# Router queries from fp32 weights and an fp32 router input instead of split halves

## The chip, the cores and the metric
The kernel runs on one core of a Trainium2 chip. The metric is the device time of one launch in microseconds. A core has five engines that work side by side, each in the order of its own instructions: TensorE (PE, with PEld for its weight loads), VectorE (DVE), ScalarE (ACT), GpSimd (POOL) and SyncE (SP), which here only issues transfers.

## The reference, cut to what matters
A hybrid encoder block (gated linear attention beside differential attention, merged, with a residual) is followed by PEER, a retrieval layer over 128 x 128 single-neuron experts. There are 256 tokens of width 2048, all in float32. The part that matters is PEER, on `xb = rmsnorm(hs, g_ffn)`:

```
qb = (xb @ w_q).reshape(TB, 8, 2, 128)              # router queries, 8 heads
s = einsum('thpc,hpnc->thpn', qb, sub_keys)         # scores of 128 keys, twice
sv, si = top_k(s, 16)
cand = sv[:, :, 0, :, None] + sv[:, :, 1, None, :]  # 16 x 16 pairs
cv, ci = top_k(cand, 16);  eidx = ...               # 16 experts of each head
g = softmax(cv)
a = gelu(einsum('thkd,td->thk', u_tab[eidx], xb))   # 128 rows of 2048 per token
out = einsum('thkd,td'..., g * a, v_tab[eidx])
```

The final output is `rmsnorm(hs + out)`.

## The kernel before
The whole program is straight-line code. A planner with a timing model of its own puts it in order ahead of the run and sets the waits, so each engine has one fixed order; blocks marked high priority are put ahead of others that are ready at the same planned time. Tiles with one tag share a few buffers.

**Projections.** `proj` computes 256 columns of a product with a 2048-row weight in two halves of 8 row blocks each, 1 MB per half. `load_half` fetches a half on SP's queue (L174), ScalarE rounds it to `hi` in fp32r (L185), and DVE, or the engine given as `lo_eng`, subtracts to get `lo` (L186). The activations are kept as the same pair of halves. PE multiplies three pairs for each block: high by high, high by low, low by high (L200 to L202), 256 token columns at a time, so 96 products for one call.

**The router.** The output projection `w_o` (L215 to L217) ends the attention part; its result `hs` is transposed on PE (L665) block by block, and `hg[k]`, the router input before its row scaling, is made as a high half by ScalarE (L667) and a low half by DVE (L668). `queries(h)` then runs for each of the eight heads: `proj` with `w_q`, ScalarE's copy to `pqt` (L783), fp32 score products with the transposed keys (L790), ScalarE's scaled copy to `s0` or `sS1` (L792), and `route(0, h)` for the first 128 tokens. For head 0 DVE makes `lo`, for heads 1 to 7 POOL. The first half of a weight lies in the `raw` tag (3 buffers); the second in the `ring` pool (3 buffers) for heads 0 and 1, in four quarter tiles of the old `s1` buffers for heads 2 to 4, and in `raw` for heads 5 to 7.

**Routing.** `route` finds the top 16 twice on DVE (L708 to L712), adds the pairs (`cand`, L723), takes the top 16 of them, and turns them into row numbers with a few small operations (`hl` L729 and L730, `ohx` L734, L736 on POOL, L737, L739). ScalarE's exponent (L743) takes `cv`.

**Lookups.** `gather_dots` fetches one row of the `u` table for each of 128 tokens, 1 MB, with an indirect transfer on POOL's queue (L751), and DVE multiplies it by `xb` and sums (L754). There are 256 of these, half into `g` tiles of `ring`, half into `gr` tiles that share the tag `raw` with the query weights. `route(1, h)` for the second 128 tokens is interleaved. `weights_of(0)` (GELU, L763) follows the last dot of the first 128 tokens; `build_w0` then builds a one-hot weight array W0 on ScalarE and PE (L815 to L821), while DVE goes on with the dots of the second 128. `split_w` makes the halves `wb` of W0 (L897, L898).

**The dense stage.** With W0 and W1 built, a product over the whole `v` table runs to the end, with the last 576 columns by gathers (L884, L887).

Of the kernel before, what the change touches and what calls it, by code (L numbers as in the profile page):

```python
# [10 lines left out]
F32 = mybir.dt.float32  # L11
F32R = mybir.dt.float32r
# [3 lines left out]
AF = mybir.ActivationFunctionType  # L16
ALU = mybir.AluOpType
# [3 lines left out]
P = 128  # L21
D = 2048
KT = D // P
T = 256
# [16 lines left out]
def block_kernel(ctx: ExitStack, tc: tile.TileContext, A: dict, out: bass.AP):  # L41
    nc = tc.nc

    def pool(name, bufs=1, space=None, side=None, c=ctx):
        kw = {}
        if space is not None:
            kw["space"] = space
        if side is not None:
            kw["side"] = side
        return c.enter_context(tc.tile_pool(name=name, bufs=bufs, **kw))  # L50
# [5 lines left out]
    wp = pool("wp", side="right", c=wpc)  # L56
# [7 lines left out]
    s2p = pool("s2p", c=ph1)  # L64
    ph0 = ExitStack()
    s1p = pool("s1p", c=ph0)

    def pm(shape=(P, N)):
        return pmain.tile(list(shape), F32, tag="pm", name="pm")

    def pa(shape):
        return paux.tile(list(shape), F32, tag="pa", name="pa")
# [76 lines left out]
    for k in range(KT):  # L149
        ps = pa([P, N])  # L150
        for i, (xt, n) in enumerate(xs):
            nc.tensor.matmul(ps[:, i * P:i * P + n], lhsT=xt[:, k * P:(k + 1) * P], rhs=sc[i], start=True, stop=True)
        g = vec[:, gm + k:gm + k + 1]
# [6 lines left out]
    def block_of(c0):  # L160
        return (c0 - 32 if c0 > OFF_LR else c0) // 256

    def load_half(w, c0, kh, ncol=256, lo_eng=None, ring=None):

        src = w[block_of(c0), kh]
        if ring is None:
            parts = [wp.tile([P, 8, ncol], F32, tag="raw", name="raw", bufs=3)]
        elif isinstance(ring, list):
            parts = [s1p.tile([P, 2, ncol], F32, tag=f"s1_{t}", name="raws") for t in ring]
        else:  # L170
            parts = [ring.tile([P, 8, ncol], F32, tag="g", name="rawg")]
        n = 8 // len(parts)
        for i, raw in enumerate(parts):
            nc.sync.dma_start(raw, src[:, i * n:(i + 1) * n, :])  # L174
        res = []
        for q in range(2):
            hi = wp.tile([P, 4, ncol], F32R, tag="hi", name="hi", bufs=3)
            lo = wp.tile([P, 4, ncol], F32R, tag="lo", name="lo", bufs=3)
            m = min(n, 4)
            with tc.high_priority():  # L180
                for i in range(4 // m):
                    k0 = 4 * q + i * m
                    raw = parts[k0 // n][:, k0 % n:k0 % n + m, :]
                    ks = slice(i * m, (i + 1) * m)
                    nc.scalar.activation(hi[:, ks], raw, AF.Copy)  # L185
                    (lo_eng or nc.vector).tensor_sub(lo[:, ks], raw, hi[:, ks].bitcast(F32))  # L186
            res.append((hi, lo))
        return res

    def proj(w, c0, act, n, evac, lo_eng=None, ring=None):  # L190

        ps = [pm((P, n)) for _ in range(2)]
        for kh in range(2):
            for q, (hi, lo) in enumerate(load_half(w, c0, kh, lo_eng=lo_eng, ring=ring and ring[kh])):
                for kk in range(4):
                    k = kh * 8 + q * 4 + kk
                    ah, al = act[k][:, 0, :n], act[k][:, 1, :n]
                    for b in range(2):
                        wh, wl = hi[:, kk, b * P:(b + 1) * P], lo[:, kk, b * P:(b + 1) * P]
                        nc.tensor.matmul(ps[b], lhsT=wh, rhs=ah, start=(k == 0), stop=False)  # L200
                        nc.tensor.matmul(ps[b], lhsT=wh, rhs=al, start=False, stop=False)  # L201
                        nc.tensor.matmul(ps[b], lhsT=wl, rhs=ah, start=False, stop=(k == KT - 1))  # L202
        for b in range(2):
            evac(b, ps[b])

    def proj_tokens(w, c0, act, evac):

        ps = [pm((P, 256)) for _ in range(2)]
        for kh in range(2):
            for q, (hi, lo) in enumerate(load_half(w, c0, kh)):  # L210
                for kk in range(4):
                    k = kh * 8 + q * 4 + kk
                    for tt in range(2):
                        ah, al = (act[k][:, i, tt * P:(tt + 1) * P] for i in range(2))
                        nc.tensor.matmul(ps[tt], lhsT=ah, rhs=hi[:, kk], start=(k == 0), stop=False)  # L215
                        nc.tensor.matmul(ps[tt], lhsT=ah, rhs=lo[:, kk], start=False, stop=False)
                        nc.tensor.matmul(ps[tt], lhsT=al, rhs=hi[:, kk], start=False, stop=(k == KT - 1))  # L217
        for tt in range(2):
            evac(tt, ps[tt])
# [9 lines left out]
    for kh in range(2):  # L229
        raw = bt.tile([P, 8, 32], F32, tag="ow", name="lraw", bufs=4)  # L230
        nc.sync.dma_start(raw, w_lr[kh])
        hi = wp.tile([P, 8, P], F32R, tag="hi", name="lhi", bufs=3)
        lo = wp.tile([P, 8, P], F32R, tag="lo", name="llo", bufs=3)
# [4 lines left out]
        for kk in range(8):  # L238
            k = kh * 8 + kk
# [82 lines left out]
    def gla_head(h):  # L322
# [19 lines left out]
        def ev_r(j):  # L342
# [6 lines left out]
            return f  # L349

        proj(w_in, OFF_GQ + h * 256, hT, T, ev_q)
        proj(w_in, OFF_GK + h * 256, hT, N, ev_k)


# [74 lines left out]
        for m in (2, 3):  # L429
# [4 lines left out]
            Qb[m] = t_  # L434

        proj(w_in, OFF_GV + h * 512, hT, N, ev_v(0))
        proj(w_in, OFF_GV + h * 512 + 256, hT, N, ev_v(1))

# [203 lines left out]
    ring = pool("ring", bufs=3, side="right", c=ringc)  # L642
# [3 lines left out]
    hg = [None] * KT  # L646
    gf = vrow["g_ffn"]
    w_o = A["c_w_out"]
    for j in range(8):
        xr = bt.tile([P, 2, 256], F32, tag=f"b{j % 2}", name="xr")  # L650
        nc.sync.dma_start(xr, A["x"][0].rearrange("(a p) c -> p a c", p=P)[:, :, j * 256:(j + 1) * 256])

        def ev_o(tt, ps, j=j, xr=xr):
            cs = slice(j * 256, (j + 1) * 256)
            nc.vector.tensor_add(hs[:, tt, cs], ps, xr[:, tt, :])
            jk = bt.tile([P, 256], F32, tag="ow", name="jk", bufs=4)
            nc.scalar.activation(jk, hs[:, tt, cs], AF.Square, accum_out=ssq[:, tt, j:j + 1])

        proj_tokens(w_o, j * 256, yT, ev_o)
        for b in range(2):  # L660
            k = 2 * j + b
            g = vec[:, gf + k:gf + k + 1]
            p2 = pa([P, T])
            for tt in range(2):
                nc.tensor.transpose(p2[:, tt * P:(tt + 1) * P], hs[:, tt, k * P:(k + 1) * P], ident)  # L665
            hg[k] = s2p.tile([P, 2, T], F32R, tag=f"s2_{k}", name=f"hg{k}")
            nc.scalar.activation(hg[k][:, 0, :], p2, AF.Copy, scale=g)  # L667
            nc.vector.scalar_tensor_tensor(hg[k][:, 1, :], p2, g, hg[k][:, 0, :].bitcast(F32), op0=ALU.mult,  # L668
                                           op1=ALU.subtract)

    for tt in range(2):
        nc.gpsimd.dma_start(xb[:, tt, :], A["g_ffn"].to_broadcast([P, D]))
# [99 lines left out]

    w_q = A["c_peer_w_q"]

    wait = [(None, ring), (None, ring), (None, [4, 5, 6, 7]), (None, [8, 9, 10, 11]), (None, [12, 13, 14, 15])] + [None] * 3
    eis = {}

    def queries(h):
        qt = bt.tile([P, 2, T], F32, tag=f"b{2 + h % 2}", name="pqt")

        def ev_pq(b, ps):
            with tc.high_priority():
                nc.scalar.activation(qt[:, b, :], ps, AF.Copy)  # L783
        proj(w_q, h * 256, hg, T, ev_pq, lo_eng=nc.vector if h == 0 else nc.gpsimd, ring=wait[h])
        s0 = rp.tile([P, 2, P], F32, tag="sS0", name="sS0", bufs=2)
        with tc.high_priority():
            for tt in range(2):
                ps = pa([P, 2, P])
                for p in range(2):
                    nc.tensor.matmul(ps[:, p, :], lhsT=qt[:, p, tt * P:(tt + 1) * P], rhs=skT[h // 2][:, 2 * (h % 2) + p, :],  # L790
                                     start=True, stop=True)
                nc.scalar.activation(s0 if tt == 0 else sS1[:, h], ps, AF.Copy, scale=rst[tt])  # L792
            eis[0, h] = route(0, h, s0)

    sub_keys(0)
    queries(0)
    for b in range(1, 4):
        sub_keys(b)
    for tt in range(2):
        nc.vector.scalar_tensor_tensor(xb[:, tt, :], hs[:, tt, :], rst[tt], xb[:, tt, :], op0=ALU.mult, op1=ALU.mult)  # L800
    for h in range(1, 8):
        queries(h)
# [250 lines left out]
```

## Time and profile before

| what | value |
|---|---|
| median of 3 runs | 2611.87 us (2609.34 to 2613.95) |
| the profiled execution | 2616.36 us, span 2614.6 us |
| PE busy | 1889.1 us (72%) |
| DVE busy | 2132.0 us (82%) |
| ACT busy | 1106.8 us (42%) |
| POOL busy | 1266.1 us (48%) |
| mean DMA rate over the span | 252 GB/s |

The busy shares are means over stages that differ: PE is busy in 90% or more of nearly every slice until about 1200 us and again from about 2000 us on, DVE from about 1200 on. The stage table among the rows below is therefore the view to start from.

### The profile page before, as it was taken

The numbers are of one execution on the slowest core, as the hardware profiler recorded it, in microseconds if no ns is written. First come the engines' busy times: TensorE is split into PE (matmuls) and PEld (weight loads), VectorE is DVE, ScalarE is ACT, GpSimd is POOL, SyncE is SP. The second block draws the span as 40 slices with busy tenths as digits, with TensorE's granted clock in tenths as the row PEclk, the third lists the DMA queues.
The fourth block names the chain that finished last, engine by engine and source line by source line (L and its number), as shares of the span: only waits on it lengthen the run. The fifth ranks groups of instructions, "written<-read, shape, count | busy, mean of one in ns | idle before, by whom it ended". The sixth has DMA issues, their size and how long they took to land. (4 is left out here: it accounts for less than half of the span.)

```text
span 2614.6 us, 37107 instructions
## 1 busy us (share of the span) xinstructions
PE 1889.1 (72%) x13809; PEld 1835.5 (70%) x13809; DVE 2132.0 (82%) x2921; ACT 1106.8 (42%) x2076; POOL 1266.1 (48%) x989
## 2 busy tenths in 40 slices
PE   8999999999999999997500000143006999999997
PEld 7999999999999999997500000132005888999897
DVE  4778877557777775559999999996978899999998
ACT  4565554345655544443200000698006344444444
POOL 1333310000110001028876888885856777777775
PEclk9999999999999999998855555566558999999999
DMA  4445445554444465656699899997993788889886
GB/s 160 146 147 178 146 148 199 187 181 164 165 157 166 167 237 180 227 198 213 227 350 347 322 375 422 421 421 298 418 357 117 263 304 301 315 302 306 302 300 240
DMA packets 110913, 658.38 MB, mean 252 GB/s; under 512 B 14514, under 2 KB 17132, under 8 KB 53116
## 3 DMA queue, kind: packets, MB, share of 16 engines
q0 software_dynamic: 59216, 348.40, 35.2%
q1 hardware_dynamic: 51312, 307.45, 33.8%
q8 instruction: 108, 1.77, 0.3%
q14 instruction: 73, 0.60, 0.1%
q10 hardware_dynamic: 204, 0.17, 0.0%
HBM read 652.78 MB, written 2.10 MB: 250 GB/s over the span
## 5 line engine op out<-in xcount | busy, mean ns | idle before, releaser
L186 DVE TENSOR_TENSOR lo<-raw,hi 128x1024 fp32r<-128x1024 f32 x354 | 453.2, 1281 | 242.7 <-ACT hi L185 240.9
L202 PE MATMUL pm<-hT,lo 128*128 128x256 f32 (+1 forms) x2048 | 577.9, 285 | 7.9 <-DVE lo L186 7.9
L200 PE MATMUL pm<-hT,hi 128*128 128x256 f32 (+1 forms) x2048 | 581.8, 285 | 0.0
L201 PE MATMUL pm<-hT,hi 128*128 128x256 f32 (+1 forms) x2048 | 581.6, 285 | 0.0
L185 ACT ACTIVATE hi<-raw 128x1024 fp32r<-128x1024 f32 x374 | 395.9, 1059 | 363.3 <-PE pm L201 292.5
L202 PEld LDWEIGHTS pm<-hT,lo 128*128 128x128 f32 x2048 | 384.9, 189 | 10.7 <-DVE lo L186 9.0
L200 PEld LDWEIGHTS pm<-hT,hi 128*128 128x128 f32 x2048 | 386.0, 188 | 0.3
L201 PEld LDWEIGHTS pm<-hT,hi 128*128 128x128 f32 x2048 | 386.1, 189 | 0.2
L884 POOL DMA_INDIRECT gv<-in_peer_v_dram,ent x256 | 309.6, 1209 | 140.9 <-DVE hs L887 87.1
L754 DVE SCALAR_TENSOR_TENSOR g<-g,xb 128x2048 f32<-128x2048 f32 x128 | 326.4, 2553 | 15.6 <-DMA g<-in_peer_u_dram,ent 15.3
L768 PE MATMUL pa<-cc,gwt 128*128 128x128 f32 x2 | 0.9, 474 | 462.3 <-DVE gwt L764 462.3
L926 PE MATMUL acc<-vhi,wb 128*128 128x368 f32 x1024 | 334.2, 331 | 0.8 <-DVE wb L898 0.8
L768 PEld LDWEIGHTS pa<-cc,gwt 128*128 128x128 f32 x2 | 0.4, 181 | 462.9 <-DVE gwt L764 462.9
L754 DVE SCALAR_TENSOR_TENSOR gr<-gr,xb 128x2048 f32<-128x2048 f32 x128 | 295.3, 2309 | 28.8 <-DMA gr<-in_peer_u_dram,ent 28.8
L887 DVE SCALAR_TENSOR_TENSOR hs<-gv,gwt,hs 128x576 f32<-128x576 f32 x256 | 280.3, 1095 | 39.3 <-DMA gv<-in_peer_v_dram,ent 35.0
L751 POOL DMA_INDIRECT gr<-in_peer_u_dram,ent x128 | 259.0, 2023 | 78.6 <-DVE gr L754 33.5
L751 POOL DMA_INDIRECT g<-in_peer_u_dram,ent x128 | 250.3, 1956 | 82.4 <-DVE g L754 31.2
L926 PEld LDWEIGHTS acc<-vhi,wb 128*128 128x128 f32 x1024 | 192.4, 189 | 1.0 <-DVE wb L898 1.0
L925 PE MATMUL acc<-vlo,wb 128*128 128x368 f32 x512 | 172.9, 342 | 18.0 <-DVE vlo L917 9.2
L925 PE MATMUL acc<-vlo,wwv 128*128 128x368 f32 x512 | 172.3, 341 | 15.0 <-DVE vlo L917 10.4
L539 POOL DMA_DIRECT2D sw<-dqT x8 | 4.5, 563 | 287.1 <-ACT dqT L552 175.0
L820 PE MATMUL pa<-oh 128*128 128x128 f32 x256 | 58.1, 408 | 104.2 <-ACT oh L819 102.8
(876 smaller groups left out, 4610.6 us busy)
## 6 DMA issues: line engine op xcount, KB each, us to landing
raw<-in_c_w_in_dram SPq DMA_DIRECT2D x128, 1024.0 KB
raw<-in_c_w_branch_gla_dram SPq DMA_DIRECT2D x16, 1024.0 KB
raw<-in_c_w_branch_diff_dram SPq DMA_DIRECT2D x16, 1024.0 KB
raw<-in_c_w_out_dram SPq DMA_DIRECT2D x16, 1024.0 KB
raw<-in_c_peer_w_q_dram SPq DMA_DIRECT2D x11, 1024.0 KB
gv<-in_peer_v_dram,ent POOLq DMA_INDIRECT x256
raws<-in_c_peer_w_q_dram SPq DMA_DIRECT2D x12, 256.0 KB
xt<-in_x_dram SPq DMA_DIRECT2D x2, 1024.0 KB
```

The source lines that it names most:

```text
L185: nc.scalar.activation(hi[:, ks], raw, AF.Copy)
L186: (lo_eng or nc.vector).tensor_sub(lo[:, ks], raw, hi[:, ks].bitcast(F32))
L200: nc.tensor.matmul(ps[b], lhsT=wh, rhs=ah, start=(k == 0), stop=False)
L201: nc.tensor.matmul(ps[b], lhsT=wh, rhs=al, start=False, stop=False)
L202: nc.tensor.matmul(ps[b], lhsT=wl, rhs=ah, start=False, stop=(k == KT - 1))
L751: nc.gpsimd.indirect_dma_start(out=g, out_offset=None, in_=u_tab, in_offset=bass.IndirectOffsetOnAxis(ap=ei[:, k:k + 1], axis=0))
L754: nc.vector.scalar_tensor_tensor(g, g, 1.0, xb[:, tt, :], op0=ALU.mult, op1=ALU.mult, accum_out=dots[tt][:, s:s + 1])
L820: nc.tensor.matmul(ps[:, q, :], lhsT=oh[:, 1, q], rhs=oh[:, 0, q], start=True, stop=True)
L884: nc.gpsimd.indirect_dma_start(out=g, out_offset=None, in_=v_tab, in_offset=bass.IndirectOffsetOnAxis(ap=eis[tt, s // 16][:, s % 16:s % 16 ...
L887: nc.vector.scalar_tensor_tensor(hs[:, tt, DC:], g, gw[tt][:, s:s + 1], hs[:, tt, DC:], op0=ALU.mult, op1=ALU.add)
L925: nc.tensor.matmul(o, lhsT=wh[:, tt, :], rhs=lo[:, ns], start=False, stop=False)
L926: nc.tensor.matmul(o, lhsT=wl[:, tt, :], rhs=hi[:, ns], start=False, stop=last(tt))
```

## The change
The query products take the weights as they are loaded, in fp32, and `hg` as one fp32 tile. The high and low halves of the query weights and the low half of `hg` are no longer made, and one fp32 product stands in the place of three fp32r ones. Loading is taken out of `load_half` into `load_raw`, with the same tags and the same order of loads. The `hi` and `lo` tags stay for the other projections.

```diff
-    def load_half(w, c0, kh, ncol=256, lo_eng=None, ring=None):
+    def load_raw(w, c0, kh, where=None):
...
+        return [(8 * kh + i * n, raw) for i, raw in enumerate(parts)]
+
+    def load_half(w, c0, kh, ncol=256):
+
+        (_, raw), = load_raw(w, c0, kh)
...
-            hg[k] = s2p.tile([P, 2, T], F32R, tag=f"s2_{k}", name=f"hg{k}")
-            nc.scalar.activation(hg[k][:, 0, :], p2, AF.Copy, scale=g)
-            nc.vector.scalar_tensor_tensor(hg[k][:, 1, :], p2, g, hg[k][:, 0, :].bitcast(F32), op0=ALU.mult,
-                                           op1=ALU.subtract)
+            hg[k] = s2p.tile([P, T], F32, tag=f"s2_{k}", name=f"hg{k}")
+            nc.scalar.activation(hg[k], p2, AF.Copy, scale=g)
...
-        proj(w_q, h * 256, hg, T, ev_pq, lo_eng=nc.vector if h == 0 else nc.gpsimd, ring=wait[h])
+        ps = [pm((P, T)) for _ in range(2)]
+        for kh in range(2):
+            for k0, raw in load_raw(w_q, h * 256, kh, wait[h][kh]):
+                for kk in range(raw.shape[1]):
+                    k = k0 + kk
+                    for b in range(2):
+                        nc.tensor.matmul(ps[b], lhsT=raw[:, kk, b * P:(b + 1) * P], rhs=hg[k], start=(k == 0), stop=(k == KT - 1))
+        for b in range(2):
+            ev_pq(b, ps[b])
```

## Rows read from the trace of the kernel before

**Rows 1.** Stages: stretch, its us, busy us of each engine, granted clock, DMA share, GB/s
```profile
1184.00:1300.00 116.00, 80.17 (x571) 76.49 (x570) 112.17 (x201) 30.55 (x57) 97.90 (x61) 0.87 0.62 216
1300.00:1656.00 356.00, 0.66 (x2) 0.29 (x2) 344.30 (x542) 5.65 (x22) 290.58 (x157) 0.50 0.95 366
1656.00:1800.00 144.00, 48.97 (x217) 43.76 (x217) 132.21 (x116) 141.45 (x398) 124.63 (x58) 0.61 1.01 421
...
1822.00:1976.00 154.00, 0.14 (x1) 0.14 (x1) 130.53 (x116) 1.07 (x3) 105.13 (x53) 0.51 0.89 352
1976.00:2614.00 638.00, 586.41 (x3329) 552.76 (x3329) 588.41 (x808) 302.17 (x505) 461.83 (x436) 0.98 0.81 277
```

**Rows 2.** Timelines of ACT and DVE: start us, us, what [idle before, releaser]
```profile
1657.57 0.31 ACT L763 ACTIVATE gwt<-gwt 128x128 f32<-128x128 f32 x1 [136.81 <-DVE gr L754]
...
1822.37 0.42 DVE L898 TENSOR_TENSOR wb<-W,wb 128x256 fp32r<-128x256 f32 x1 [21.72 <-ACT wb L897]
```

**Rows 3.** DVE by line and shape, 1184 to 1300: busy us, mean ns
```profile
L754 DVE SCALAR_TENSOR_TENSOR g<-g,xb 128x2048 f32<-128x2048 f32 x16 | 66.1, 4134 | 2.8 <-DMA g<-in_peer_u_dram,ent 2.8
L734 DVE TENSOR_TENSOR ohx<-hlf,cc 128x512 f32<-128x512 f32 x5 | 7.1, 1416 | 0.0
L723 DVE TENSOR_TENSOR cand<-sv 128x256 f32<-128x256 f32 x6 | 6.3, 1051 | 0.0
...
L729 DVE TENSOR_SCALAR hl<-ci 128x16 uint32<-128x16 uint32 x5 | 3.0, 598 | 0.0
```

**Rows 4.** DVE by line and shape, 1300 to 1540
```profile
L754 DVE SCALAR_TENSOR_TENSOR g<-g,xb 128x2048 f32<-128x2048 f32 x38 | 91.0, 2396 | 0.0
...
L734 DVE TENSOR_TENSOR ohx<-hlf,cc 128x512 f32<-128x512 f32 x10 | 6.9, 687 | 1.2 <-POOL hlf L732 0.9
...
L723 DVE TENSOR_TENSOR cand<-sv 128x256 f32<-128x256 f32 x9 | 3.8, 423 | 0.0
...
L729 DVE TENSOR_SCALAR hl<-ci 128x16 uint32<-128x16 uint32 x10 | 1.5, 153 | 0.0
```

**Rows 5.** POOL by line and shape, 1150 to 1300
```profile
L186 POOL TENSOR_TENSOR lo<-raw,hi 128x1024 fp32r<-128x1024 f32 x20 | 54.2, 2715 | 7.8 <-ACT hi L185 7.7
```

**Rows 6.** Timelines of POOL and DVE, start of the lookups
```profile
1170.70 0.49 DVE L708 MAX8 sv<-sS 128x8 f32<-128x128 f32 x2 [8.49 <-ACT sS L792]
...
1185.21 1.31 POOL L751 DMA_INDIRECT g<-in_peer_u_dram,ent  x1 [0.17 <-issue]
...
1191.02 7.71 DVE L754 SCALAR_TENSOR_TENSOR g<-g,xb 128x2048 f32<-128x2048 f32 x1 [2.80 <-DMA g<-in_peer_u_dram,ent]
...
1194.03 2.55 POOL L186 TENSOR_TENSOR lo<-raws,hi 128x512 fp32r<-128x512 f32 x2
```

**Rows 7.** Timeline of PE, products of 256 columns: two fp32, four fp32r
```profile
264.26 0.82 PE L449 MATMUL pa<-Qf-1_2664,ksf 128*16 128x256 f32 x3
...
264.26 1.04 PE L449 MATMUL pa<-Qf-1_2664,ksf 128*16 128x256 f32 x4
...
1165.75 0.28 PE L200 MATMUL pm<-hg,hi 128*128 128x256 f32 x1
...
1168.45 0.28 PE L200 MATMUL pm<-hg,hi 128*128 128x256 f32 x1
...
1290.07 0.41 PE L200 MATMUL pm<-hg,hi 128*128 128x256 f32 x1
1290.28 0.41 PE L201 MATMUL pm<-hg,hi 128*128 128x256 f32 x1
```

**Rows 8.** Tiles `hg` and `pqt`: ns min/median/max, first and last start us
```profile
L200 PE MATMUL pm<-hg,hi x256: 277/281/561, 1150.0 to 1295.4; 128*128 128x256 f32 x128
...
L790 PE MATMUL pa<-skT,pqt x64: 270/275/583, 1168.6 to 1297.0; 128*128 128x128 f32 x64
```

**Rows 9.** Stage table and PE's timeline, one wait for `pqt`
```profile
1246.00:1262.00 16.00, 6.26 (x46) 6.06 (x47) 15.90 (x23) 2.01 (x6) 9.69 (x8) 0.76 0.73 263
...
1260.71 1.22 PE L790 MATMUL pa<-skT,pqt 128*128 128x128 f32 x4 [8.39 <-ACT pqt L783]
```

More of the change, by code (lines that the diff above doesn't have):

```diff
@@ L161, in block_of @@
         return (c0 - 32 if c0 > OFF_LR else c0) // 256
-    def load_half(w, c0, kh, ncol=256, lo_eng=None, ring=None):
+    def load_raw(w, c0, kh, where=None):
         src = w[block_of(c0), kh]
[L166 to L169, printed above, removed]
+        if where is None:
+            parts = [wp.tile([P, 8, 256], F32, tag="raw", name="raw", bufs=3)]
+        elif isinstance(where, list):
+            parts = [s1p.tile([P, 2, 256], F32, tag=f"s1_{t}", name="raws") for t in where]
         else:
-            parts = [ring.tile([P, 8, ncol], F32, tag="g", name="rawg")]
+            parts = [where.tile([P, 8, 256], F32, tag="g", name="rawg")]
         n = 8 // len(parts)
@@ L178, in load_half, with proj @@
             lo = wp.tile([P, 4, ncol], F32R, tag="lo", name="lo", bufs=3)
-            m = min(n, 4)
             with tc.high_priority():
[L181 to L186, printed above, removed]
+                src = raw[:, 4 * q:4 * q + 4, :]
+                nc.scalar.activation(hi, src, AF.Copy)
+                nc.vector.tensor_sub(lo, src, hi.bitcast(F32))
             res.append((hi, lo))
         return res
-    def proj(w, c0, act, n, evac, lo_eng=None, ring=None):
+    def proj(w, c0, act, n, evac):
         ps = [pm((P, n)) for _ in range(2)]
         for kh in range(2):
-            for q, (hi, lo) in enumerate(load_half(w, c0, kh, lo_eng=lo_eng, ring=ring and ring[kh])):
+            for q, (hi, lo) in enumerate(load_half(w, c0, kh)):
                 for kk in range(4):
@@ L773, in block_kernel @@
     w_q = A["c_peer_w_q"]
-    wait = [(None, ring), (None, ring), (None, [4, 5, 6, 7]), (None, [8, 9, 10, 11]), (None, [12, 13, 14, 15])] + [None] * 3
+    wait = [(None, ring), (None, ring), (None, [4, 5, 6, 7]), (None, [8, 9, 10, 11]), (None, [12, 13, 14, 15])] + [(None, None)] * 3
     eis = {}
```

## The prediction, made before the changed kernel was run
> **What bounds the kernel now.** I read the stage table first. Between 1184 and 1976 us the table lookups of the retrieval stage run, and the engine at work is DVE: 112 of 116 us in the first stretch, 344 of 356 in the next, while PE is nearly idle from 1300 on [rows 1]. From 1656 to 1800 the DMA share is 1.01 at 421 GB/s and DVE waits a little for each gathered tile: there the gathers set the pace. After 1976 a dense stage of 638 us follows, in which the changed code has no part.
>
> Next, the handovers. The exact GELU of token tile 0 starts at 1657.57 (call this T0, the time at which the dot products of tile 0 are done). ScalarE then builds W0 from it, and DVE, which works in program order, stands for 21.72 us at 1822.37 before `wb` [rows 2]. So what comes after T0 hangs on T0: if T0 moves, the building of W0, that wait, the last dots and the dense stage move with it. The question is what the change does to T0.
>
> Then DVE by line and shape, in two stretches. From 1184 to 1300, while the queries are still computed, a dot product on a `g` tile takes 4134 ns, `ohx` 1416, `cand` 1051 and the shift to `hl` 598 [rows 3]. From 1300 to 1540, with no query left, the same operations on the same shapes take 2396, 687, 423 and 153 [rows 4]. What differs is POOL: up to 1300 it makes the low halves of the query weights, 2715 ns each for the largest shape [rows 5]. The timeline shows the two together: the dot that begins at 1191.02 lasts 7.71 us, and POOL's `lo` pair of 1194.03 lies within it [rows 6]. DVE is thus held up by POOL's subtractions where it is already full.
>
> PE in the query stage: an fp32r product of 256 columns follows the one before after 0.117 us (2.70 us over 23 intervals), and an instruction of an fp32 product of 256 columns after 0.22 (1.04 for four against 0.82 for three) [rows 7]. The score products are fp32 already: 32 in the code, 64 in the trace [rows 8]. One fp32 product is two instructions.
>
> **The change part by part.**
> *Removed from DVE, ScalarE and POOL.* POOL loses its `lo` subtractions for heads 1 to 7, in work 7 x 4 of the 1024-wide size; DVE loses the four of head 0 and the 16 low halves of `hg`, ScalarE the high halves. The last three lie before DVE's first score at 1170.70, ahead of which it has 8.49 us of idle time [rows 6], or on ScalarE, busy 31 of 116 us [rows 1]: nothing on the path. Were that cover gone, the 16 small DVE operations would come back in the projection ahead, where PE sets the pace.
> *DVE freed from POOL.* Dots: 16 x (4.134 - 2.396) = 27.8 us. Routing: `cand` 6 x (1.051 - 0.423) = 3.8, `ohx` 5 x (1.416 - 0.687) = 3.6, `hl` 5 x (0.598 - 0.153) = 2.2; together 9.6 [rows 3, 4]. The value after is a measured one, in a stretch where POOL still issues gathers and does its part of the routing. Bounds: 0, if the tiles come no faster (a rival), to 37.4 in all.
> *PE.* A head has 96 fp32r instructions now (3 x 256 over eight heads) and 64 fp32 ones then: 96 x 0.117 = 11.3 us against 64 x 0.22 = 14.1. With the score products about 15.2 us a head, so from the start at 1150.0 the eighth is done at 1150 + 8 x 15.2 = 1272, against the last score product of before at 1297.0 [rows 8]. PE does more work and still ends sooner, since it now waits for POOL's halves. Its 2.9 us more for each head are covered by DVE's gathers; without gathers to do, they would cost up to 8 x 2.9 = 23 us.
> The Trainium skill, "FP8 and Floating Point Precision", section "TensorE Precision Notes", speaks against the change here: true FP32 is four passes through the array, where the present form makes three. Four passes at the row's 0.117 would be 0.468 us a product and 15.0 us a head rather than 14.1; nothing else in the sum would move.
> *Start.* The first score is ready after 14.1 us of products and about 1 of transposes, near 1165, against 1168.6 [rows 8]. The first routing then is free of POOL's queue, so the first gather goes out about 7 us before 1185.21 and the first dot starts about 7 before 1191.02 [rows 6]. But the second head's scores come no sooner than now (1150 + 2 x 15.2, plus 2 for copies, is 1182), so about 6 us of its routing move from before the first dot to behind it. Net 1 us; bounds -6 and +7.
> *Loads.* The weight loads keep their order on SP's queue and their buffers. A weight buffer comes free when PE has read it, not when POOL has. One `g` buffer needs 5.8 us from issue to first use [rows 6], a dot of 2.4 and about 1.4 to be issued again, so three buffers give a tile each 3.2 us. DVE takes one each (15.2 - 6) / 2.4 = 3.8 per head, or 4.0 us. If the landing takes 2.4 us longer next to the weight loads, that margin is gone; I take off 4 us for starved dots, from bounds of 0 and 28.
> Sum: 27.8 + 9.6 + 1 - 4 = 34.4 us, all before T0 and so carried to the end. The profiled execution took 2616.36, so 2582 in its place. The runs' median is 4.5 us below it: 2578.
>
> **The rivals.**
> *A, slower: PE at its low clock.* `pqt` is copied by ScalarE in order, behind the exponent of the head before, which waits for DVE's routing; PE's score products wait for `pqt` (8.39 us at 1260.71) and the granted clock of that stretch is 0.76, a mixture of 1.2 and 2.4 GHz [rows 9]. At 1.2 GHz the products are 0.21 us apart instead of 0.117 [rows 7], so an fp32 head would be 64 x 0.44 = 28 and with scores 30 us. If four of eight heads run so, the last score comes at 1150 + 4 x 15.2 + 4 x 30 = 1331, 34 us after 1297; DVE, in order, stands before that routing, and the time is about 2612 + 34 = 2646. It decides from the third slow head on: with two, 1150 + 6 x 15.2 + 2 x 30 = 1301, the time of before. For it: DVE takes its order from a plan made ahead. Against it: the waits for POOL that made PE idle go away, and DVE's part of a head, which the exponent waits for, shrinks by 37.4 / 7 = 5 us.
> *B: the gathers come no faster.* Three `g` buffers serve the stretch; if gathers land later beside the weight loads, the 27.8 us become waits for DMA. Left are 9.6 + 1, so 2601. For it: 4.0 against 3.2 us is a thin margin. Against it: the stretch moves 216 GB/s, and 421 are reached later [rows 1].
> *C: one ceiling for all loads.* 1184 to 1800 moves 25 + 130 + 61 = 216 MB [rows 1]. If the loads could do no more than the 352 GB/s of the last gather stretch, those bytes would take 614 us of the present 616, and next to nothing could be won: 2610. The row at 421 GB/s over 144 us speaks against it. The Trainium skill, "SBUF — State Buffer", section "A bandwidth-pool intuition that's wrong (but worth ruling out)", gives about 358 GB/s between HBM and one core, by which 216 MB take 603 us and at most 13 could be won; this trace's 421 contradicts it.
> *D: a better order.* The instruction order is planned anew for the whole program. If `wb` falls behind the end of W0, its 21.72 us go too: 2578 - 22 = 2556. Nothing in the profile asks for it.
> *E: POOL is not what stretches the dots*, and nothing is won: 2612. Against it is the overlap in [rows 6].
>
> **How the numbers follow.** The forecast has 0.62, A 0.12, B 0.13, C 0.02, D 0.07, E 0.04. The predicted time is the forecast's, 2578. The range goes from D's 2556 to 2606, past B's 2601 with some microseconds for a later start; it leaves out A, C, E and the edges. About 0.2% (5 us) is what a measurement of this kernel can tell from no change. Faster: 0.62 + 0.13 + 0.07, less 0.02 for B with a poor start, is 0.80. Same: C, E and those 0.02, 0.08. Slower: A, 0.12.
>
> **What would show it.** In the profile after: no `lo` of POOL between 1150 and 1300; dots on `g` near 2.4 us from the first; 512 products of `hg` 0.22 us apart at a granted clock near 1.00; the last score product near 1272; T0 near 1623 and the 21.72 us wait still there. Long waits of DVE for the score copies with a clock near 0.5 would show A, waits of the dots for their DMA B. The prediction is wrong if T0 moves and the end doesn't, or if the order behind T0 changes.

## The result and the profile after

The changed kernel takes 2584.56 us (median of 5 runs, 2580.14 to 2586.63) against 2612.36 for the kernel before, measured beside it: a ratio of 0.9892, 95% interval 0.9878 to 0.9907. It is 27.8 us faster; 34.4 was forecast. Measured a second time (`changed_again`), the ratio was 0.9887 (0.9871 to 0.9904). Below, each kernel is compared by its ratio to the kernel before that was measured beside it, and differences of ratios are given as microseconds of 2612.

First the stage table of the changed kernel (stretch, its us, busy us and count of PE, PEld, DVE, ACT and POOL, granted clock, DMA share, GB/s). It answers to [rows 1]; the stretches are those of the same work, so their edges lie a little earlier.

```profile
1182.00:1281.00 99.00, 91.53 (x447) 80.20 (x446) 81.65 (x197) 12.46 (x38) 42.07 (x39) 1.00 0.81 306
1281.00:1510.00 229.00, 0.66 (x2) 0.29 (x2) 228.01 (x447) 3.60 (x18) 157.69 (x102) 0.50 0.91 337
...
1651.00:1817.00 166.00, 59.16 (x259) 53.10 (x259) 132.21 (x119) 162.40 (x451) 126.23 (x59) 0.60 0.94 390
1817.00:1948.00 131.00, 0.00 (x0) 0.00 (x0) 113.82 (x101) 0.73 (x2) 73.44 (x45) 0.50 0.91 358
1948.00:2582.00 634.00, 587.89 (x3329) 556.15 (x3329) 582.27 (x809) 302.65 (x505) 456.00 (x438) 0.97 0.81 278
```

POOL was busy for 97.90 of 116 us while the queries ran and is now for 42.07 of 99. PE has changed places with it: 91.53 of 99, at a granted clock of 1.00. DVE was full (112.17 of 116) and now is not: it stands idle for 17.4 of 99 us. The groups of DVE in that stretch say why (line, engine, operation, names, shapes, count | busy us, mean ns | idle before and its releaser); they answer to [rows 3].

```profile
L753 DVE SCALAR_TENSOR_TENSOR g<-g,xb 128x2048 f32<-128x2048 f32 x21 | 51.2, 2440 | 15.0 <-DMA g<-in_peer_u_dram,ent 15.0
L733 DVE TENSOR_TENSOR ohx<-hlf,cc 128x512 f32<-128x512 f32 x5 | 3.4, 678 | 0.6 <-POOL hlf L731 0.5
L722 DVE TENSOR_TENSOR cand<-sv 128x256 f32<-128x256 f32 x5 | 3.1, 624 | 0.0
...
L728 DVE TENSOR_SCALAR hl<-ci 128x16 uint32<-128x16 uint32 x5 | 0.8, 165 | 0.1
```

A dot takes 2440 ns instead of 4134, and the 15.0 us of waiting for `g` tiles (2.8 before) are the new cost. The next rows are the tiles of PE (ns min/median/max, first and last start) and, below them, three rows of the timelines of DVE and POOL; they answer to [rows 8] and [rows 6].

```profile
L789 PE MATMUL pm<-hg,raw x352: 378/379/382, 1152.6 to 1275.1; 128*128 128x256 f32 x176
L789 PE MATMUL pm<-hg,raws x96: 379/379/379, 1191.1 to 1227.2; 128*128 128x256 f32 x96
L789 PE MATMUL pm<-hg,rawg x64: 379/379/382, 1160.4 to 1183.1; 128*128 128x256 f32 x64
...
L797 PE MATMUL pa<-skT,pqt x64: 272/275/377, 1171.6 to 1280.1; 128*128 128x128 f32 x64
```

```profile
1172.83 0.49 DVE L707 MAX8 sv<-sS 128x8 f32<-128x128 f32 x2 [13.71 <-ACT sS L799]
...
1182.94 1.09 POOL L750 DMA_INDIRECT g<-in_peer_u_dram,ent  x1 [1.81 <-issue]
...
1188.68 2.29 DVE L753 SCALAR_TENSOR_TENSOR g<-g,xb 128x2048 f32<-128x2048 f32 x1 [6.61 <-DMA g<-in_peer_u_dram,ent]
```

512 instructions make the fp32 products (352 + 96 + 64), and the score products end at 1280, 17 us before those of the kernel before. Yet the first routing begins 2.1 us later and the first dot only 2.3 us earlier. Last the two rows that answer to [rows 2], from the timelines of ScalarE and DVE.

```profile
1651.46 0.31 ACT L762 ACTIVATE gwt<-gwt 128x128 f32<-128x128 f32 x1 [134.74 <-DVE gr L753]
...
1816.50 0.42 DVE L905 TENSOR_TENSOR wb<-W,wb 128x256 fp32r<-128x256 f32 x1 [21.64 <-ACT wb L904]
```

T0 came 6 us earlier, and so did `wb`, with its wait unchanged. So the gain did not travel by T0. It is there all the same when dots are counted in the timelines: the 142nd dot, at which the kernel before reaches T0, begins at 1655.23 before and at 1631.69 after, 23.5 us earlier. The order made for the changed kernel puts 149 dots ahead of T0 instead of 142 (7 more dots of tile 1), and so 50 instead of 57 are left behind `wb`. That last part takes 131.3 us instead of 153.1.

DVE's stage row from its first routing operation to the end of the last dot balances the account; first the kernel before, then the changed one, then a second profile of the changed one (`changed_again`).

```profile
1170.70:1975.50 804.80, 152.89 (x946) 142.86 (x944) 729.56 (x1014) 207.24 (x547) 631.20 (x334) 0.59 0.87 343
```

```profile
1172.80:1947.80 775.00, 160.55 (x756) 141.78 (x754) 695.54 (x1014) 183.32 (x518) 525.50 (x304) 0.59 0.91 357
```

```profile
1172.40:1957.30 784.90, 161.35 (x757) 142.37 (x754) 695.72 (x1014) 183.37 (x519) 535.73 (x304) 0.59 0.90 353
```

The same 1014 operations take 34.0 us less (729.56 to 695.54), idle time grows from 75.2 to 79.5, and the start is 2.1 later: 34.0 - 4.2 - 2.1 = 27.7. The dense stage is 4.6 us shorter (639.1 to 634.5), so these two executions differ by 32.3 in all.

That 27.7 is so near the gain of the medians is luck, as the second profile shows. It has the same busy time, and up to the 236th dot the same times (that dot begins at 1909.1 before, at 1885.5 and 1886.0 in the two profiles of the changed kernel). Then its last dots wait longer for their gathers and end 9.5 us later: 33.8 - 13.9 - 1.7 = 18.2 us. Its dense stage is shorter by nearly as much (626.8 us), so the two executions differ by only 1.8 us in all. The 34 us of DVE's operations and the lead of some 23 us are therefore firm; the edge between the lookups and the dense stage is uncertain by some 10 us in one profile. Over the profiles of the study the dense stage takes 627 to 642 us; why it varies is open.

### The profile page after: what moved, and what is told of

Same layout as the page of the kernel before. It is cut to its first block, busy times and chain, and to the rows that moved or that the text cites. A ratio compares the mean times of both kernels' runs of the same rounds, so it can differ in the third digit from the quotient of the medians.

```text
span 2582.3 us, 36449 instructions
## 1 busy us (share of the span) xinstructions
PE 1900.4 (74%) x13553; PEld 1838.1 (71%) x13553; DVE 2078.5 (80%) x2901; ACT 1075.2 (42%) x2038; POOL 1143.0 (44%) x955
## 5 line engine op out<-in xcount | busy, mean ns | idle before, releaser
L186 ACT ACTIVATE hi<-raw 128x1024 fp32r<-128x1024 f32 x352 | 372.6, 1059 | 334.8 <-PE pm L202 273.6
L891 POOL DMA_INDIRECT gv<-in_peer_v_dram,ent x256 | 303.7, 1186 | 139.8 <-DVE hs L894 92.1
L753 DVE SCALAR_TENSOR_TENSOR g<-g,xb 128x2048 f32<-128x2048 f32 x128 | 300.3, 2349 | 24.8 <-DMA g<-in_peer_u_dram,ent 24.8
L750 POOL DMA_INDIRECT g<-in_peer_u_dram,ent x128 | 231.2, 1806 | 135.1 <-DVE g L753 59.1
L750 POOL DMA_INDIRECT gr<-in_peer_u_dram,ent x128 | 234.8, 1834 | 96.3 <-DVE gr L753 50.5
L932 PE MATMUL acc<-vlo,wb 128*128 128x368 f32 x512 | 171.7, 343 | 16.5 <-DVE vlo L926 11.2
```

The lines of the kernel that those rows point to most:

```text
L186: nc.scalar.activation(hi, src, AF.Copy)
L750: nc.gpsimd.indirect_dma_start(out=g, out_offset=None, in_=u_tab, in_offset=bass.IndirectOffsetOnAxis(ap=ei[:, k:k + 1], axis=0))
L753: nc.vector.scalar_tensor_tensor(g, g, 1.0, xb[:, tt, :], op0=ALU.mult, op1=ALU.mult, accum_out=dots[tt][:, s:s + 1])
L891: nc.gpsimd.indirect_dma_start(out=g, out_offset=None, in_=v_tab, in_offset=bass.IndirectOffsetOnAxis(ap=eis[tt, s // 16][:, s % 16:s % 16 ...
L932: nc.tensor.matmul(o, lhsT=wh[:, tt, :], rhs=lo[:, ns], start=False, stop=False)
```

## The experiments

**Is it POOL's subtractions, and is it what they read?** Two kernels put work back on POOL in the changed kernel, into a tile that nobody uses. The first puts back a subtraction that reads the raw tile (heads 1 to 7); the second, three fills of the same size that read nothing.

```diff
             for k0, raw in load_raw(w_q, h * 256, kh, wait[h][kh]):
+                for i in range(0, raw.shape[1] if h else 0, 4):
+                    m = min(4, raw.shape[1])
+                    lo = wp.tile([P, 4, 256], F32R, tag="lo", name="lo", bufs=3)    # F32 for the fills
+                    with tc.high_priority():
+                        nc.gpsimd.tensor_sub(lo[:, :m], raw[:, i:i + m], raw[:, i:i + m])   # pool_subs_back
+                        for _ in range(3): nc.gpsimd.memset(lo[:, :m], 0.0)                 # pool_memsets instead
...
```

> The changed kernel, with POOL subtracting each query weight of heads 1 to 7 from itself into the old low-half tile; nothing reads the result. PE keeps its fp32 products. Port theory (POOL's two-input subtractions stretch DVE): dots of the query stage go back to 3.5 to 4.1 us each, and 20 to 30 us of the gain are lost, about 2605 to 2615. Rival (the gain is PE's, which no longer waits for halves): PE waits for nothing of this, so the time stays at 2585.

> The changed kernel, with three memsets by POOL over the same tile in the place of each subtraction: POOL is about as busy but reads nothing. Port theory: dots stay at 2.3 to 2.6 us, and what is lost is only what POOL's queue delays the gathers, 0 to 10 us: 2585 to 2595. Queue theory (it is POOL's full queue that costs, whatever runs there): as much is lost as with the subtractions, 2605 and more.

Subtractions: 2605.39, ratio 0.9971 (0.9960 to 0.9982), so 20.6 us of the gain are gone, give or take 5. Fills: 2588.98, ratio 0.9906 (0.9885 to 0.9928), 3.7 us, with the intervals of the two kernels overlapping. The groups of DVE with the subtractions, from 1182 to 1282, and the stage row:

```profile
L753 DVE SCALAR_TENSOR_TENSOR g<-g,xb 128x2048 f32<-128x2048 f32 x18 | 45.9, 2552 | 2.2 <-DMA g<-in_peer_u_dram,ent 2.2
L728 DVE TENSOR_SCALAR hl<-ci 128x16 uint32<-128x16 uint32 x5 | 7.7, 1536 | 0.0
L722 DVE TENSOR_TENSOR cand<-sv 128x256 f32<-128x256 f32 x5 | 6.8, 1363 | 0.0
L738 DVE SCALAR_TENSOR_TENSOR ent<-ijt 128x16 int32<-128x16 f32 x3 | 5.3, 1767 | 0.0
...
1182.00:1282.00 100.00, 90.70 (x433) 79.45 (x432) 90.14 (x186) 10.46 (x34) 61.69 (x50) 0.96 0.75 279
```

and with the fills, DVE's dots, its shift to `hl` and the stage row:

```profile
L753 DVE SCALAR_TENSOR_TENSOR g<-g,xb 128x2048 f32<-128x2048 f32 x19 | 44.3, 2334 | 9.4 <-DMA g<-in_peer_u_dram,ent 8.6 <-PE pm L795 0.8
...
L728 DVE TENSOR_SCALAR hl<-ci 128x16 uint32<-128x16 uint32 x5 | 1.9, 379 | 0.1
...
1182.00:1282.00 100.00, 88.63 (x433) 78.30 (x431) 80.59 (x203) 11.36 (x36) 90.00 (x93) 0.94 0.80 297
```

With the fills POOL is busy for 90.00 of 100 us, about as in the kernel before, and a dot still takes 2334 ns. With the subtractions it is busy for only 61.69, and the loss is over five times as large. So neither POOL's being busy nor its queue holds DVE up, but what it does there: the two kinds of work differ in that one reads SBUF, and so also waits for its weights. The loss came as the first theory had it, but not on the dots, which take 2552 ns and not the expected 3.5 to 4.1 us. The subtractions stretch what they fall on: in this order mostly the small operations (`hl` 165 ns in the changed kernel, 1536 here), in the kernel before the dots. Over the whole lookup stage DVE is busy for 712.0 us instead of 695.5, and of these 16.5 us 16.3 lie on `hl`, `ent` and `cand`. The Trainium skill, "SBUF — State Buffer", section "Who interferes with whom", says this of a DVE operation with two SBUF inputs: it contends with a GpSimd operation that reads SBUF, not with one that only writes there. The two runs agree for the dots, `cand` and `ent`, which have two inputs: 20.6 against 3.7 us. The shift to `hl` has one input, so that sentence does not cover it, and the fills stretch it too (379 ns against 165). Each edited kernel is also ordered anew, which no run separates from the edit itself.

**Is fp32 needed for that, or would DVE do?** In the kernel before, only the engine of the low halves was changed; nothing is fp32 that was not.

```diff
-        proj(w_q, h * 256, hg, T, ev_pq, lo_eng=nc.vector if h == 0 else nc.gpsimd, ring=wait[h])
+        proj(w_q, h * 256, hg, T, ev_pq, lo_eng=nc.vector, ring=wait[h])
```

> The kernel before with only the engine of the low halves changed: DVE makes those of all heads, POOL none. POOL's contention is gone, DVE has 28 subtractions of 1024 columns more; DVE's own of that size in the projection ahead are the measure of one. Theory 'POOL's reads stretch DVE': the dots of 1184 to 1300 take near 2.4 us, cand about 0.6, and the 28 subtractions at 1.1 to 1.3 us take 31 to 36 us of DVE, so it comes out level: 2603 to 2618. Theory 'the dots are long for another reason (weights landing, PE reading)': they stay above 3 us and the time is 30 us and more above the kernel before: 2640 and above.

2589.31, ratio 0.9905 (0.9880 to 0.9930). The dots are short, as the first theory had it, but neither has the time: it wins 24.8 us and can't be told from the changed kernel. DVE's groups from 1184 to 1300, and PE's tile:

```profile
L754 DVE SCALAR_TENSOR_TENSOR g<-g,xb 128x2048 f32<-128x2048 f32 x19 | 43.3, 2279 | 4.6 <-DMA g<-in_peer_u_dram,ent 4.6
L186 DVE TENSOR_TENSOR lo<-raw,hi 128x1024 fp32r<-128x1024 f32 x16 | 22.0, 1381 | 0.0
L754 DVE SCALAR_TENSOR_TENSOR gr<-gr,xb 128x2048 f32<-128x2048 f32 x7 | 17.0, 2427 | 0.0
L186 DVE TENSOR_TENSOR lo<-raws,hi 128x512 fp32r<-128x512 f32 x8 | 5.2, 684 | 0.0
```

```profile
L790 PE MATMUL pa<-skT,pqt x64: 270/275/546, 1167.5 to 1263.9; 128*128 128x128 f32 x64
```

DVE makes 27.2 us of halves here and still 26 dots by 1300, where the kernel before makes 17 and the changed kernel 27. Part of the work falls where DVE would wait for tiles (the changed kernel waits 15.0 us). And PE, with the shorter fp32r products, ends the scores at 1264 instead of 1280, so that the raw buffers go to the gathers sooner (7 `gr` dots by 1300; the changed kernel has 2, the first at 1287). What counted was to take POOL's subtractions off; the fp32 form and the halves on DVE then pay about the same, one in PE's time and the other in DVE's.

**Where does the starving come from?** Gathers have three `g` buffers, and the three `raw` ones only when the query weights leave them, last those of heads 5 to 7. Here those weights go into the quarter tiles that heads 2 to 4 used.

```diff
-    wait = [... (None, [12, 13, 14, 15])] + [(None, None)] * 3
+    wait = [... (None, [12, 13, 14, 15]), ([4, 5, 6, 7], [8, 9, 10, 11]), ([12, 13, 14, 15], [4, 5, 6, 7]), ([8, 9, 10, 11], [12, 13, 14, 15])]
```

> The changed kernel, with the six weight halves of heads 5 to 7 in the quarter tiles that heads 2 to 4 leave, not in the three buffers that half of the gathers use. Supply theory (DVE's 15 us of waits for gathered tiles in the query stage come from having only the three g buffers): gr gathers start in the query stage, those waits fall below 5 us, and the time goes to 2570 to 2577. Rival (the waits come from POOL's gathers standing in its queue behind routing work that waits for DVE): no change, 2582 to 2587.

2566.50, ratio 0.9829 (0.9805 to 0.9853): 16.5 us better than the changed kernel, a little more than expected. DVE's dots and the stage row, 1182 to 1282:

```profile
L753 DVE SCALAR_TENSOR_TENSOR g<-g,xb 128x2048 f32<-128x2048 f32 x14 | 31.9, 2281 | 7.4 <-DMA g<-in_peer_u_dram,ent 7.3
L753 DVE SCALAR_TENSOR_TENSOR gr<-gr,xb 128x2048 f32<-128x2048 f32 x10 | 22.8, 2282 | 1.5 <-DMA gr<-in_peer_u_dram,ent 1.5
...
1182.00:1282.00 100.00, 85.96 (x422) 75.29 (x420) 93.03 (x224) 11.15 (x34) 47.43 (x42) 0.97 0.92 358
```

DVE is busy for 93 of 100 us. The other way to free the buffers is to end the products sooner; this kernel leaves out every second row block of the query products, so its result is not the reference's.

```diff
-                for kk in range(raw.shape[1]):
+                for kk in range(0, raw.shape[1], 2):
...
-                        nc.tensor.matmul(... stop=(k == KT - 1))
+                        nc.tensor.matmul(... stop=(k == KT - 2))
```

> The changed kernel with every second row block left out of the query products, so that PE has 32 fp32 instructions a head for 64 and the queries are not the reference's; loads, routing and gathers keep their number. Covered theory (PE's pace is hidden behind DVE's gathers): only the earlier first score counts, 4 to 9 us: 2576 to 2581. PE theory (a head's 14 us set the pace of the stage): 7 us for each of eight heads, 2530 to 2545.

2561.07, ratio 0.9804 (0.9784 to 0.9825), 23 us better than the changed kernel and between the two theories. The stage row of 1182 to 1282 shows DVE full and PE, with its work halved, done early (last scores at 1219.9).

```profile
1182.00:1282.00 100.00, 32.66 (x157) 28.26 (x155) 99.57 (x255) 9.23 (x30) 53.03 (x46) 0.67 0.92 354
```

So the pace of the fp32 products costs up to 23 us of the change's possible gain; that it does so by holding raw buffers and the scores is argued. The better placement gives back 16.5 without touching the products.

**The same with halves, and with subtractions.** Three kernels cross the placement with who makes the halves: the kernel before with it (`halves_freed`), `raw_freed` with POOL's subtractions put back (`freed_subs`), and halves on DVE with it (`lo_on_dve_freed`). The edits are the ones shown.

> The kernel before (halves, three products, subtractions on POOL) with one thing changed: the weights of heads 5 to 7 land in the quarter tiles that the heads before them used, so the three raw buffers are left to the gathers. The queries' arithmetic is the kernel before's. Theory 'supply and POOL are two costs': without the fp32 change the raw buffers alone win a part, since the dots of this stretch are still stretched by POOL's subtractions (above 3 us on average from 1182 to 1300) and the queries end near 1297: 5 to 15 us below the kernel before. Theory 'the buffers were all': the placement alone wins what it won behind the change, about 18 us, and the time is near 2594 or below. Theory 'the placement is worth something only behind the change': within 3 us of the kernel before.

> raw_freed (fp32 queries, the weights of heads 5 to 7 in quarter tiles) with POOL's subtractions of heads 1 to 7 put back, each reading a raw tile and writing a tile that nobody uses. Theory 'POOL's reads cost DVE time by themselves': the subtractions cost about the 21 us that they cost behind the plain change, whatever the supply: 2583 to 2590. Theory 'they cost mostly by holding raw tiles and POOL's queue, and so the supply': with more buffers they cost under 10 us: 2567 to 2576.

> halves_lo_on_dve (halves kept, DVE makes all low halves) with the weights of heads 5 to 7 in quarter tiles, as in raw_freed. It tells what the fp32 products themselves are worth once tiles are not short. Theory 'the change won by freeing DVE of POOL, and the fp32 form pays only where DVE is full': here DVE has tiles all the time, so its 33 us of subtractions displace dots and the time stays well above raw_freed's 2566.5, at 2580 to 2597. Theory 'fp32 is worth nothing beside POOL': shorter products free the buffers sooner and make up for the subtractions: 2562 to 2572.

> The changed kernel itself, unaltered, beside the others of this call: 2580 to 2589, a ratio of 0.988 to 0.991 to the kernel before. If it lies elsewhere, differences of under 5 us between runs of different calls say nothing.

| ratio to the kernel before | usual buffers | raw buffers freed |
|---|---|---|
| halves, lows on POOL | 1 (the kernel before) | 0.9946 (0.9930 to 0.9962) |
| halves, lows on DVE | 0.9905 (0.9880 to 0.9930) | 0.9866 (0.9849 to 0.9882) |
| fp32, subtractions put back on POOL | 0.9971 (0.9960 to 0.9982) | 0.9880 (0.9858 to 0.9902) |
| fp32, POOL free | 0.9892 (the change) | 0.9829 (0.9805 to 0.9853) |

The placement alone, with POOL's subtractions in place, wins 14 us: supply and contention are two costs. With more buffers the subtractions cost 13 us (0.9829 to 0.9880, give or take 8 from the two intervals), between the two theories by ratio, though the time, 2583.41, lies at the lower edge of the first one's range. DVE's stage rows tell them apart: `pool_subs_back`, `raw_freed` and `freed_subs`, from the first routing operation to the end of the last dot.

```profile
1169.90:1961.50 791.60, 162.96 (x757) 143.60 (x755) 712.01 (x1015) 182.99 (x519) 557.09 (x325) 0.59 0.89 350
...
1167.30:1930.90 763.60, 160.97 (x757) 142.37 (x755) 693.94 (x1014) 183.53 (x519) 576.97 (x304) 0.60 0.91 362
...
1169.70:1945.30 775.60, 162.88 (x757) 144.31 (x755) 713.78 (x1014) 183.77 (x519) 582.92 (x338) 0.59 0.90 357
```

The subtractions add 16.5 us to DVE's busy time with the usual buffers (695.54 to 712.01) and 19.8 with the freed ones (693.94 to 713.78; 16.5 of these on the dots, which they meet in that order). The two profiles of the changed kernel give this busy time alike to 0.2 us. So what the subtractions cost DVE does not shrink with more buffers, which speaks for the first theory; in `freed_subs` part of it falls into waits (idle 61.8 us, 69.7 in `raw_freed`). And with buffers to spare, where DVE has little idle time to give in that stretch, the fp32 form beats halves on DVE by 10 us (0.9829 against 0.9866, give or take 8); beside the usual buffers the two can't be told apart.

**Rival D's price.** In `raw_freed`, the first `wb` was tied to a late dot; the order made from this puts all dots ahead of it.

```diff
   with tc.high_priority():
+      if g == 0:
+          nc.vector.tensor_copy(wl[:, 0, 0, 0:1], dots[1][:, 88:89])
```

> raw_freed with one more order: the first wb of the dense stage is tied to a late dot product, so that DVE does the dots that are left before it waits for W0. Theory 'the 22 us wait is lost time' (rival D's price): the wait at wb goes and the time falls by 12 to 22 us from raw_freed's 2566.5, to 2545 to 2555. Theory 'the gathers, not DVE, set the pace there': while DVE waits, only the few buffers fill, so most of the wait is a true loss; but if the loads of the dense stage then come later, the dense stage gives 5 to 15 back: 2556 to 2566.

2552.17, ratio 0.9764 (0.9739 to 0.9790), 17 us below `raw_freed`, give or take 9, 62 us below the kernel before, and the fastest kernel of the study. On DVE's timeline nothing waits for W0 any more; first `raw_freed`, then this kernel:

```profile
1761.74 0.42 DVE L905 TENSOR_TENSOR wb<-W,wb 128x256 fp32r<-128x256 f32 x1 [22.13 <-ACT wb L904]
```

```profile
1914.15 0.15 DVE L903 CAST wb<-gwt 128x1 fp32r<-128x1 f32 x1 [0.38 <-ACT gwt L762]
1914.22 0.28 DVE L763 TENSOR_TENSOR gwt<-gwt 128x128 f32<-128x128 f32 x1
1914.62 0.43 DVE L907 TENSOR_TENSOR wb<-W,wb 128x256 fp32r<-128x256 f32 x1
```

The last dots end 16.7 us earlier than in `raw_freed` (1930.9 to 1914.2), and the dense stage takes 636 us against 633. Of the 22 us of waiting, about 17 were lost time.

## Why the prediction was right, and where it was not

*Dots, 27.8 forecast.* Over all 256 dots DVE's busy time fell by 23.6 us. Before and after, the groups of the whole lookup stage:

```profile
L754 DVE SCALAR_TENSOR_TENSOR g<-g,xb 128x2048 f32<-128x2048 f32 x128 | 326.4, 2553 | 15.6 <-DMA g<-in_peer_u_dram,ent 15.3
L754 DVE SCALAR_TENSOR_TENSOR gr<-gr,xb 128x2048 f32<-128x2048 f32 x128 | 295.3, 2309 | 28.8 <-DMA gr<-in_peer_u_dram,ent 28.8
```

```profile
L753 DVE SCALAR_TENSOR_TENSOR g<-g,xb 128x2048 f32<-128x2048 f32 x128 | 300.3, 2349 | 24.8 <-DMA g<-in_peer_u_dram,ent 24.8
L753 DVE SCALAR_TENSOR_TENSOR gr<-gr,xb 128x2048 f32<-128x2048 f32 x128 | 297.8, 2329 | 25.9 <-DMA gr<-in_peer_u_dram,ent 25.9
```

The mechanism held; this term was mis-sized by 4.2. It fell short because the dots outside the 16 stretched ones grew a little, from 2315 ns ((621.7 - 66.1) / 240) to 2336 on the mean of all 256. POOL still has one product with two SBUF inputs for each routing, and either engine can be the one that waits, as these rows of DVE and POOL in the changed kernel show:

```profile
1234.05 2.29 DVE L753 SCALAR_TENSOR_TENSOR g<-g,xb 128x2048 f32<-128x2048 f32 x1
...
1234.21 3.25 POOL L735 TENSOR_TENSOR ohx<-ohx,sif 128x512 f32<-128x512 f32 x1 [0.24 <-DVE ohx L733]
...
1279.80 1.26 POOL L735 TENSOR_TENSOR ohx<-ohx,sif 128x512 f32<-128x512 f32 x1 [0.81 <-DVE ohx L733]
...
1280.04 3.18 DVE L753 SCALAR_TENSOR_TENSOR g<-g,xb 128x2048 f32<-128x2048 f32 x1
```

At 1234 the dot was first and POOL's product took 3.25 us instead of 1.26; at 1280 POOL was first and the dot took 3.18 instead of 2.29. Counted over the timelines, such meetings make up the whole shortfall. Above the median dot (2293 ns before, 2291 after), the 12 dots that overlap a subtraction carry 27.6 us before, and there are none after; the others that overlap POOL's product carry 8.7 us before and 13.1 after, 4.4 more; the rest carry nothing, to 1 us.

*Routing, 9.6.* Measured 9.6 over the stage: `ohx` 14.6 to 11.0 us, `cand` 11.7 to 7.9, the first `hl` 4.7 to 2.5.

*Start, +1.* It was -2.1. The stage's first product starts 2.6 us later (1152.6), and the first scores wait on PE's queue: `pqt` is ready at 1167.9, but 17 instructions of the next head still go ahead of the scores, which begin at 1171.6, 3.7 us later. The prediction counted 1 us there. A head takes the 15.2 us that it gave ((1275.1 - 1152.6) / 8 = 15.3), with 64 x 0.216 = 13.8 of products, nearer to its 14.1 than to its 15.0 for four passes; with the later start and the queue the last score came at 1280 instead of 1272.

*PE's longer heads, put at nothing.* The prediction let DVE's gathers cover them. `half_products` gains 23 us from shorter ones, so PE's pace was not covered; what the 2.9 us of a head cost by themselves no run shows.

*Starved dots, 4 taken off.* Over the whole stage idle time grew by 4.2 us, but the step's picture was wrong. In the first stretch it grew by 13.5 (17.4 against 3.8): a gather took a median of 7.9 us to land beside the weight loads, not the 5.8 that the first one of before showed, so three buffers give a tile each (7.9 + 2.4 + 1.4) / 3 = 3.9 us, which is the 4.0 that DVE wants, with no margin left for its uneven demand. Up to `wb` 10.0 of it were left (52.3 to 62.3 us of idle time). Behind `wb`, where DVE waits for tiles again and now has fewer dots to do, it shrank in this profile (22.9 us of 153.1 before, 17.2 of 131.3 after), but not in the second one, whose idle time of the whole stage is 13.9 above the kernel before. The net 4.2 agrees with the 4 by luck; `raw_freed` and `half_products` show that 16 to 23 us were to be had there.

*"All before T0 and so carried to the end".* This step failed: T0 moved by 6 us, not 34. A new order put 7 dots of tile 1 ahead of T0, and the lead showed behind `wb`. The prediction had named a changed order behind T0 as a sign that it is wrong, and in this step it is. The sum survives it, since DVE is what the whole lookup stage runs on and has the same 1014 operations to do.

So in the first profile the 34.4 became 27.7 by two terms: the freed operations (34.0 instead of 37.4) and the start (-2.1 instead of +1). In the second, more starving took it to 18.2, and a dense stage 12.3 us shorter than before, which the prediction left as it was, made up for it.

*The rivals.* A did not come: the products ran at a granted clock of 1.00 from 1182 to 1281. B was half right: its 15.0 us of waiting are there, but the freed time was worth more. C needed a ceiling of 352 GB/s: the changed kernel moved 390 from 1651 to 1817, and `freed_wb_behind` 371 over its whole lookup stage, waits included. D did not come by itself (21.64 us of waiting are still there); made by hand in `raw_freed` it was worth about 17, not 22. E is refuted by the subtractions put back: they stretch DVE's operations, and in the order of `freed_subs` these are the dots.

## What to carry to other kernels

Before replacing an operation to relieve an engine, ask which part of it hurts: here a one-word change (low halves on DVE) wins as much as the fp32 products, as far as the runs can tell, and the crossing of four variants shows where the two part. When the busy engine is freed, look at once at what feeds it, with the landing time measured under the new load and not in a quiet stretch. Measure a lead by counting the bound engine's finished operations, since a landmark such as T0 moves with the order, and profile a kernel twice before a stage's last microseconds are explained.

## What the runs showed of the hardware

- POOL's subtractions hold DVE up, fills of the same size hardly: a dot takes 2334 ns beside POOL that is 90% busy with fills (4134 in [rows 3]). Of DVE's small operations the shift to `hl`, `cand` and `ent` are stretched by the subtractions (1536, 1363 and 1767 ns), the maxima and index searches are not (285 and 286 ns). POOL's own product stretches `cand` too: 1.50 us at 1249.29 in `raw_freed`, beside a product that began at 1249.22.
- An fp32 product of 256 columns is two instructions, 0.216 us apart at a granted clock of 1.00 (18 of them in 4.05 us, of which 0.38 are the last one's own). Two are 0.43 us, 3.7 times the 0.117 of an fp32r product.
- A gather of 1 MB into a `g` tile lands in a median of 7.9 us at a DMA share of 0.81 (1182 to 1281 of the changed kernel) and in 10.9 at 0.92 (`raw_freed`, with the raw buffers gathering too): the share rises, the single gather gets slower, and more of them in flight still win.
